# Differential attention: score products over all 128 rows, with stacked hi and lo parts, and the values of the second half among the first heads

## The chip, the cores and the metric

One core of a Trainium2 chip runs the whole kernel in one launch. The metric is the device time of that launch in microseconds (us), the median of several runs. All inputs lie in the chip's memory before the launch.

## The reference

A decoder of two layers on 512 positions with 1024 features in f32: swiglu half steps and a gated convolution in the first layer, then keys and values projected once from the residual, then a second layer with causal differential attention over them. The change touches only the attention.

```python
def diff_attention(h, k, v, w_q, lq1, lk1, lq2, lk2, g_subln, w_o, lambda_init):
    q = (h @ w_q).reshape(b, s, N_HEADS, 2, HEAD_DIM) * (HEAD_DIM ** -0.5)
    ...
    scores = jnp.einsum("bqhcd,bkhcd->bhcqk", qb, k).astype(f32)
    ...
    p = jax.nn.softmax(jnp.where(causal, scores, -jnp.inf), axis=-1)
    a = p[:, :, 0] - lam * p[:, :, 1]
    return jnp.einsum("bhqk,bkhe->bqhe", a.astype(v.dtype), v)
    ...
    o = rms_norm(o, g_subln) * (1.0 - lambda_init)
    return o.reshape(b, s, D_MODEL) @ w_o
```

There are 8 heads. Each has two components (index c) of 64 dimensions, two sets of scores and two softmaxes, whose difference is applied to values of 128 columns.

## The kernel before, in words

Activations are held transposed: features on the 128 partitions, the 512 positions along the free axis. Every f32 product is made of three matmuls of a faster type (fp32r): each operand is split into a rounded part (hi) and the rest (lo), and hi x hi, hi x lo and lo x hi are added up in PSUM. `split` (L133 on, its copy at L138 on ScalarE, its subtraction at L141 on VectorE) makes the two parts of an activation, `unit` those of a weight block: SP starts a load of 512 KB into one of two `raw` buffers (L127), ScalarE casts it to whi (L128), VectorE subtracts for wlo (L129). There are seven pairs of such buffers (`WUNITS`). `products` (L143 on) issues the three matmuls, L147 to L149.

The attention's body (L589 on) is written for one head n of eight at a time, and its functions are these. `values(half, tts)` multiplies the activations by half of the value weights, for position tiles tts (L618 to L620, 24 matmuls of 512 columns for each tile). Half 0 serves heads 0 to 3, half 1 heads 4 to 7. `keys(n, k0, k1)` makes the keys of head n, 24 matmuls of 512 columns in all, called in two halves, and at the end splits them. `queries(n)` splits the queries. `scores(n, qt)` (L639 on) makes both components' scores of the query tile qt against (qt + 1) x 128 keys: for each component three matmuls of 64 rows (L653), the first component from partitions 0 to 63, the second from 64 to 127, then a matmul that adds the mask (L655), the row maximum (`top`, L656), the exponential with its sum (L661), the reciprocal (L662) and the mixing of the two components (L665, L666) into `e`. `turn(n, qt)` transposes it on TensorE (tr, L678) and splits the result into aT. `attend(n)` multiplies by the values (L689 to L691), copies the result to `q` and squares it (osq, L694). `sub_norm(n)` adds up the squares on TensorE (otot, L698) and normalizes.

A pool `ps` of six PSUM buffers holds every sum, a pool `pst` of two the transposes and otot.

The order of the work is the order of the calls in the loop over n, except that a scheduler, when the kernel is built, may move instructions of an engine against each other; what each engine runs is then fixed. TensorE runs its instructions strictly in that order, so a matmul that waits holds all behind it. For n = 1 to 6 the calls are: half of the keys of n+1, scores(n,2), turn(n,3), attend(n-1), the other half of the keys, scores(n,1), scores(n,0), sub_norm(n-1), turn(n,2), scores(n+1,3), turn(n,1), turn(n,0). Both halves of the values and the keys of head 0 come before the loop.

Of the kernel before, what the change touches and what calls it, by code (L numbers as in the profile page):

```python
# [9 lines left out]
F32 = mybir.dt.float32  # L10
F32R = mybir.dt.float32r
# [6 lines left out]
P = 128  # L18
D = 1024
S = 512  # L20
FF = 2816
NK = D // P
NF = FF // P
NH = 8
HD = 64
# [11 lines left out]
TEMPS = 4  # L37
HALF_TEMPS = 6
RAW = 2
WARM = 9  # L40
LAMBDA_INIT = 0.8 - 0.6 * math.exp(-0.3 * 1)
MASKED = -3.0e38
# [3 lines left out]
def yoco_kernel(ctx: ExitStack, tc, i, out):  # L46
    nc = tc.nc

    const = ctx.enter_context(tc.tile_pool(name="const", bufs=1))
    xpool = ctx.enter_context(tc.tile_pool(name="xpool", bufs=1))  # L50
    apool = ctx.enter_context(tc.tile_pool(name="apool", bufs=5 * NK))
    wsp = ctx.enter_context(tc.tile_pool(name="wsp", bufs=WUNITS))
    wraw = ctx.enter_context(tc.tile_pool(name="wraw", bufs=RAW))
    mpool = ctx.enter_context(tc.tile_pool(name="mpool", bufs=1))
# [4 lines left out]
    def slot(dtype, name):  # L59
        return apool.tile([P, S], dtype, tag="a", name=name)  # L60
# [485 lines left out]
    def attention(l, h, pn, xkv):  # L546
# [23 lines left out]
        NB = S // P  # L570
# [18 lines left out]
        def body(after, then):  # L589
# [14 lines left out]

            vu = {}

            def values(half, tts):
                accs = {tt: ps.tile([P, S], F32, tag="ps", name="v_acc") for tt in tts}
                for kk in range(NK // 2):
                    if (half, kk) not in vu:  # L610
                        vu[half, kk] = unit(i["wv"][half][:, kk * 1024 : (kk + 1) * 1024], 1024)
                    uh, ul = vu[half, kk]
                    for j in range(2):
                        k = 2 * kk + j
                        for tt in tts:
                            ah, al = (z[:, tt * P : (tt + 1) * P] for z in hkv[k])
                            wh, wl = (z[:, j * S : (j + 1) * S] for z in (uh, ul))
                            nc.tensor.matmul(accs[tt], ah, wh, start=k == 0, stop=False)  # L618
# [6 lines left out]
            kacc, ku, kq, aT, mixed, pv = {}, {}, {}, {}, {}, {}  # L625

            def keys(n, k0, k1):
                if k0 == 0:
                    kacc[n] = ps.tile([P, S], F32, tag="ps", name="k_acc")
                    ku[n] = unit(i["wk"][n], 1024)  # L630
                for k in range(k0, k1):
                    products(kacc[n], [cols(ku[n], k) + tuple(hkv[k])], k == 0, k == NK - 1)
                if k1 == NK:
                    split(kq[n][2], kq[n][3], kacc[n])

            def queries(n):
                hi, lo = pair_of_units("kq")
                kq[n] = [hi[:, :S], lo[:, :S], hi[:, S:], lo[:, S:]]
                split(kq[n][0], kq[n][1], qs[n])  # L639

            def scores(n, qt):

                qh, ql, kh, kl = kq[n]
                w = (qt + 1) * P
                qq = slice(qt * P, w)
                top, neg, sums, inv = (
                    small.tile([P, 2], F32, tag=z, name=z) for z in ("top", "neg", "sums", "inv")
                )
                sc = [ps.tile([P, S], F32, tag="ps", name="sc")[:, :w] for _ in range(2)]
                for j, (q, k) in enumerate(((qh, kh), (qh, kl), (ql, kh))):  # L650
                    for cc, s in enumerate(sc):
                        r = slice(cc * HD, (cc + 1) * HD)
                        nc.tensor.matmul(s, q[r, qq], k[r, :w], start=j == 0, stop=False)  # L653
                for cc, s in enumerate(sc):
                    nc.tensor.matmul(s[:, qt * P :], ident16, mask, start=False, stop=True)  # L655
                    nc.vector.tensor_reduce(top[:, cc : cc + 1], s, axis=AX.X, op=ALU.max)  # L656
# [25 lines left out]
            def attend(n):  # L682
                oacc = ps.tile([P, S], F32, tag="ps", name="oacc")
                e0 = (n % 4) * P
                for j in range(NB):
                    vh, vl = (z[:, e0 : e0 + P] for z in v[n // 4, j])
                    ah, al = (block(z, j, j) for z in aT[n])
                    q = slice(j * P, S)
                    nc.tensor.matmul(oacc[:, q], vh, ah, start=j == 0, stop=False)  # L689
                    nc.tensor.matmul(oacc[:, q], vh, al, start=False, stop=False)  # L690
                    nc.tensor.matmul(oacc[:, q], vl, ah, start=False, stop=j == NB - 1)  # L691
                nc.scalar.copy(qs[n], oacc)
                pv[n] = temp(S, "osq")
                nc.scalar.square(pv[n], qs[n])  # L694
# [11 lines left out]
            def normed(*ns):  # L706
                for n in ns:
                    on.append(parts_of("on"))
                    split(*on[n], qs[n])

            values(0, range(NB))
            queries(0)
            keys(0, 0, NK)
            values(1, range(NB))
            scores(0, 3)
            for n in range(NH):
                more = n < NH - 1
                if more:
                    queries(n + 1)
                    keys(n + 1, 0, 4)  # L720
                scores(n, 2)
                if not more:
                    normed(4, 5)
# [1 line left out]
                turn(n, 3)  # L725
                if n > 0:
                    attend(n - 1)
                if more:
                    keys(n + 1, 4, NK)
                else:  # L730
                    wo.begin(0, range(4, 6))
                scores(n, 1)
                scores(n, 0)
# [124 lines left out]
```

## Time and profile before

| | us |
|---|---|
| median of 3 runs | 1916.08 (1915.59 to 1917.01) |
| profiled execution | 1916.25 |
| its span | 1914.5 |
| busy TensorE (PE) / its weight loads (PEld) | 1895.8 / 1602.9 |
| busy VectorE (DVE) / ScalarE (ACT) | 993.3 / 739.5 |
| the stage from the first values to the first scores of head 0 | 49.31 |
| heads 0 to 6, from scores(n,3) to scores(n+1,3) | 97.31 |

The profile comes from one execution on the chip. Busy time is the time in which an engine has an instruction in work. The ends of matmuls are modelled, so that what counts between two matmuls is the distance of their starts. In a group's row, "x56" is the number of instructions, then come their busy time, the mean length of one in ns, and the idle time ahead of them with what ended most of it. Heads 0 to 6 are 1480.02 minus 1382.71 in the windows of the trace.

### The profile page before, as it was taken

The page shows a single profiled execution, that of the slowest core. Times are in us where ns is not written, and L with a number is a line of the kernel's source. Part 1 is how long each engine was busy: PE and PEld are TensorE (multiplying, and loading weights), DVE is VectorE, ACT ScalarE, POOL GpSimd, SP SyncE. Part 2 cuts the span into 40 slices and gives each one's busy share as a digit, 9 for nine tenths or more (in the row PEclk, how much of TensorE's full clock was granted, in tenths as well). Part 3 has the DMA queues.
Part 4 walks back from the last instruction along what each step waited for, and adds up shares of the span by engine and source line. Part 5 has one row for each costly group of instructions (what it writes and reads, how often), then busy time and mean ns, then how long its engine had stood idle before and what let it go on. Part 6 is the DMA issues. An engine that isn't in the chain of part 4 may idle for free.

```text
span 1914.5 us, 24288 instructions
## 1 busy us (share of the span) xinstructions
PE 1895.8 (99%) x9780; PEld 1602.9 (84%) x9780; DVE 993.3 (52%) x1673; ACT 739.5 (39%) x1250; POOL 1.1 (0%) x8
## 2 busy tenths in 40 slices
PE   9999999999999999999999999999999999999998
PEld 8888888988898888888988888899866898888886
DVE  7423434574566334344862443457389594234345
ACT  7322222453354322222633222335289673332132
POOL 0000000000000000000000000000000000000000
PEclk9999999999999999999999999999999999999999
DMA  5432323233323323232133332322211224233331
GB/s 167 121 102 90 106 88 103 74 95 94 112 75 104 106 87 101 90 109 89 66 114 100 103 99 95 89 87 92 74 34 61 73 67 132 78 98 100 98 90 65
DMA packets 53664, 178.45 MB, mean 93 GB/s; under 512 B 6320, under 2 KB 9520, under 8 KB 53552
## 3 DMA queue, kind: packets, MB, share of 16 engines
q1 hardware_dynamic: 51632, 174.89, 29.5%
q10 hardware_dynamic: 1920, 2.02, 0.3%
q8 instruction: 77, 1.26, 0.3%
q14 instruction: 35, 0.29, 0.1%
HBM read 174.79 MB, written 2.10 MB: 92 GB/s over the span
## 4 chain that ended last, share of the span: by engine, by line
PE 89%; DVE 7%; ACT 3%; DMA 1%; issue 1%; SPq 0%; DVEq 0%; ACTq 0%
PE acc L147 26%; PE acc L148 26%; PE acc L149 26%; PE d_acc L359 2%; PE d_acc L358 2%; PE d_acc L360 2%; DVE h_lo L221 1%; DVE d L242 1%; DVE x L243 1%; PE v_acc L618 1%; PE v_acc L620 1%; PE v_acc L619 1%; DMA raw<-in_wg 1%; ACT e L661 1%; DVE top L656 1%
## 5 line engine op out<-in xcount | busy, mean ns | idle before, releaser
L147 PE MATMUL acc<-h_hi,whi 128*128 128x512 f32 (+1 forms) x1952 | 697.6, 358 | 4.4 <-ACT whi L128 2.6
L148 PE MATMUL acc<-h_lo,whi 128*128 128x512 f32 (+1 forms) x1952 | 697.6, 358 | 0.1
L149 PE MATMUL acc<-h_hi,wlo 128*128 128x512 f32 (+1 forms) x1952 | 696.3, 357 | 0.0
L128 ACT CAST whi<-raw 128x1024 fp32r<-128x1024 f32 (+2 forms) x336 | 334.4, 1019 | 867.5 <-PE acc L148 718.7
L129 DVE TENSOR_TENSOR wlo<-raw,whi 128x1024 fp32r<-128x1024 f32 (+2 forms) x336 | 396.2, 1182 | 238.8 <-ACT whi L128 237.6
L147 PEld LDWEIGHTS acc<-h_hi,whi 128*128 128x128 f32 x1952 | 367.1, 188 | 59.4 <-ACT whi L128 2.8
L148 PEld LDWEIGHTS acc<-h_lo,whi 128*128 128x128 f32 x1952 | 367.6, 188 | 54.1 <-DVE h_lo L221 0.3
L149 PEld LDWEIGHTS acc<-h_hi,wlo 128*128 128x128 f32 x1952 | 367.3, 188 | 53.7
L410 DVE TENSOR_TENSOR gs<-acc,r 128x512 f32<-128x512 f32 (+1 forms) x100 | 62.5, 625 | 443.8 <-PE acc L149 443.7
L148 PE MATMUL acc<-act_lo,whi 128*128 128x512 f32 (+1 forms) x624 | 223.7, 359 | 0.0
L149 PE MATMUL acc<-act_hi,wlo 128*128 128x512 f32 (+1 forms) x624 | 223.2, 358 | 0.0
L147 PE MATMUL acc<-act_hi,whi 128*128 128x512 f32 (+1 forms) x624 | 223.1, 358 | 0.0
L148 PEld LDWEIGHTS acc<-act_lo,whi 128*128 128x128 f32 x624 | 117.8, 189 | 18.4
L147 PEld LDWEIGHTS acc<-act_hi,whi 128*128 128x128 f32 x624 | 117.4, 188 | 18.0
L149 PEld LDWEIGHTS acc<-act_hi,wlo 128*128 128x128 f32 x624 | 117.3, 188 | 17.7
L138 ACT CAST act_hi<-us 128x512 fp32r<-128x512 f32 (+1 forms) x100 | 56.5, 568 | 64.3 <-DVE us L414 64.3
L358 PE MATMUL d_acc<-whi,act_hi 128*128 128x512 f32 x176 | 68.4, 390 | 0.0
L359 PE MATMUL d_acc<-whi,act_lo 128*128 128x512 f32 x176 | 68.4, 389 | 0.0
L360 PE MATMUL d_acc<-wlo,act_hi 128*128 128x512 f32 x176 | 68.4, 389 | 0.0
L412 DVE TENSOR_TENSOR us<-acc,r 128x512 f32<-128x512 f32 (+1 forms) x100 | 62.5, 625 | 0.0
L141 DVE TENSOR_TENSOR act_lo<-us,act_hi 128x512 fp32r<-128x512 f32 (+1 forms) x100 | 61.7, 620 | 0.7 <-ACT act_hi L138 0.7
L414 DVE TENSOR_TENSOR us<-us,gs 128x512 f32<-128x512 f32 (+1 forms) x100 | 61.5, 620 | 0.4
(156 smaller groups left out, 1646.8 us busy)
## 6 DMA issues: line engine op xcount, KB each, us to landing
raw<-in_wg SPq DMA_DIRECT2D x85, 512.0 KB, 3.8
raw<-in_wu SPq DMA_DIRECT2D x85, 512.0 KB, 3.4
raw<-in_wd SPq DMA_DIRECT2D x48, 448.0 KB, 3.4
raw<-in_wd SPq DMA_DIRECT2D x24, 512.0 KB, 3.8
raw<-in_wci SPq DMA_DIRECT2D x24, 512.0 KB, 3.5
raw<-in_wdt SPq DMA_DIRECT2D x22, 512.0 KB, 3.7
raw<-in_wco SPq DMA_DIRECT2D x8, 512.0 KB, 3.5
raw<-in_wq SPq DMA_DIRECT2D x8, 512.0 KB, 3.4
```

Source lines behind the costliest of these rows:

```text
L128: casts.append(nc.scalar.copy(hi[:, z], raw[:, z]).ins)
L129: nc.vector.tensor_tensor(lo[:, z], raw[:, z], hi.bitcast(F32)[:, z], op=ALU.subtract)
L141: nc.vector.tensor_tensor(dst_lo, src, dst_hi.bitcast(F32), op=ALU.subtract)
L147: nc.tensor.matmul(acc, wh, ah, start=first and j == 0, stop=False)
L148: nc.tensor.matmul(acc, wh, al, start=False, stop=False)
L149: nc.tensor.matmul(acc, wl, ah, start=False, stop=last and j == n - 1)
L358: nc.tensor.matmul(acc, ah, wh, start=k == 0, stop=False)
L359: nc.tensor.matmul(acc, al, wh, start=False, stop=False)
L360: nc.tensor.matmul(acc, ah, wl, start=False, stop=k == m1 - m0 - 1)
L410: nc.vector.tensor_tensor(gs, g, r2[:, p:q], op=ALU.mult)
L412: nc.vector.tensor_tensor(us, up, r2[:, p:q], op=ALU.mult)
L414: nc.vector.tensor_tensor(us, us, gs, op=ALU.mult)
```

## The change

Scores. Instead of three matmuls of 64 rows for each component, there are two of 128 rows. The fixed operand has q_hi of that component on partitions 0 to 63 and q_lo on 64 to 127; the moving operand has k_hi on both halves in its first 512 columns and k_lo on both halves in its second 512. So two matmuls give hi x hi + lo x hi and hi x lo + lo x lo: the product of the two lo parts, left out before, is now there. The stacks are made by transfers from SBUF to SBUF that SP issues (`move`): five for the keys of a head, in two rounds, since the last two overwrite what the first three read, and three for its queries. A head's keys then take two of the seven pairs of weight buffers' tiles as `kk`, and the queries take slots of `apool`, which grows from 40 to 48; `attend` writes into a new slot instead of `q`.

Order. keys(0) come ahead of values(0). The values of the second half are made one position tile at a time in heads 0 to 3: in heads 0 to 2 behind the second half of the keys, in head 3 at its start. Queries of six heads are split and moved ahead of the loop, the others in heads 0 and 1. In heads 4 to 6 all 24 key products stand at the head's start.

```diff
             def keys(n, k0, k1):
...
                 if k1 == NK:
-                    split(kq[n][2], kq[n][3], kacc[n])
+                    a, b = kk[n] = pair_of_units("kk")
+                    split(a[:, :S], a[:, S:], kacc[n])
+                    move(b[up], a[low])
+                    for dst, src in ((b[low], a[low]), (a[low], a[up])):
+                        move(dst[:, :S], src[:, S:])
+                        move(dst[:, S:], src[:, :S])
 
             def queries(n):
-                hi, lo = pair_of_units("kq")
-                kq[n] = [hi[:, :S], lo[:, :S], hi[:, S:], lo[:, S:]]
-                split(kq[n][0], kq[n][1], qs[n])
+                hi, lo = slot(F32R, "qhi"), qs[n].bitcast(F32R)
+                split(hi, lo, qs[n])
+                both = slot(F32R, "qboth")
+                move(both[up], hi[low])
+                move(both[low], lo[low])
+                move(hi[low], lo[up])
+                xs[n] = hi, both
 
             def scores(n, qt):
...
-                for j, (q, k) in enumerate(((qh, kh), (qh, kl), (ql, kh))):
-                    for cc, s in enumerate(sc):
-                        r = slice(cc * HD, (cc + 1) * HD)
-                        nc.tensor.matmul(s, q[r, qq], k[r, :w], start=j == 0, stop=False)
+                for cc, s in enumerate(sc):
+                    for j in range(2):
+                        nc.tensor.matmul(s, xs[n][cc][:, qq], kk[n][cc][:, j * S : j * S + w], start=j == 0, stop=False)
...
+            value_weights(0)
+            keys(0, 0, NK)
+            for n in range(AHEAD // 2):
+                queries(n)
             values(0, range(NB))
-            queries(0)
-            keys(0, 0, NK)
-            values(1, range(NB))
+            for n in range(AHEAD // 2, AHEAD):
+                queries(n)
             scores(0, 3)
             for n in range(NH):
                 more = n < NH - 1
+                if n == 0:
+                    value_weights(1)
+                if n == 3:
+                    values(1, [n])
                 if more:
-                    queries(n + 1)
                     keys(n + 1, 0, 4)
+                if n < NH - AHEAD:
+                    queries(n + AHEAD)
+                if n > 3 and more:
+                    keys(n + 1, 4, NK)
                 scores(n, 2)
...
-                if more:
+                if n <= 3:
                     keys(n + 1, 4, NK)
-                else:
+                if n < 3:
+                    values(1, [n])
+                if not more:
                     wo.begin(0, range(4, 6))
```

The scheduler gives some calls other places than before. On TensorE at the end of head 0, before (tr_11255 is tile 2 of head 0, tr_11287 its tile 1; sc_11265 and sc_11266 are scores(1,3), sc_11323 scores(1,2); k_acc_11300 the keys of head 2):

```order
L653 MATMUL sc_11265<-kqhi_11131 128x512
L678 MATMUL tr_11255<-ident_7887,e_11171 128x128 x3
L653 MATMUL sc_11266<-kqhi_11131 128x512
L653 MATMUL sc_11265<-kqlo_11132,kqhi_11131 128x512
...
L147 MATMUL k_acc_11300<-h_hi_10692,whi_11302 128x512
...
L149 MATMUL k_acc_11300<-h_hi_10698,wlo_11303 128x512
L653 MATMUL sc_11323<-kqhi_11131 128x384
L678 MATMUL tr_11287<-ident_7887,e_11220 128x128 x2
```

So scores(1,3) and half of the keys of head 2 stand ahead of the transposes of tile 1. The same place after the change (sc_11196 is the second component of scores(0,0), tr_11215, tr_11245 and tr_11250 are tiles 2, 1 and 0, sc_11225 and sc_11226 scores(1,3), k_acc_11254 the keys of head 2):

```order
L671 MATMUL sc_11196<-mask_7894,ident16_7892 128x128
L694 MATMUL tr_11215<-ident_7887,e_11099 128x128 x3
L694 MATMUL tr_11245<-ident_7887,e_11182 128x128 x2
L694 MATMUL tr_11250<-ident_7887,e_11206 128x128
L669 MATMUL sc_11225<-kkhi_11129,qhi_10859 128x512 x2
L669 MATMUL sc_11226<-kklo_11130,qboth_10862 128x512 x2
...
L150 MATMUL k_acc_11254<-h_hi_10692,whi_11256 128x512
```

All three transposes have moved ahead of scores(1,3). At the end of head 3, before (sc_11841 and sc_11842 are scores(4,3), tr_11831 is tile 2 of head 3, tr_11863 tile 1, otot_11820 the norm's sum of head 2):

```order
L698 MATMUL otot_11820<-osq_11752,half128_92 128x512
L678 MATMUL tr_11831<-ident_7887,e_11720 128x128 x3
L653 MATMUL sc_11841<-kqhi_11680 128x512
L653 MATMUL sc_11842<-kqhi_11680 128x512
...
L147 MATMUL k_acc_11876<-h_hi_10692,whi_11878 128x512
...
L653 MATMUL sc_11899<-kqhi_11680 128x384
L678 MATMUL tr_11863<-ident_7887,e_11785 128x128 x2
```

and after (otot_11862, the transposes of tiles 2, 1 and 0, and sc_11883 and sc_11884, which are scores(4,3)):

```order
L715 MATMUL otot_11862<-osq_11791,half128_92 128x512
L694 MATMUL tr_11873<-ident_7887,e_11758 128x128 x3
L694 MATMUL tr_11903<-ident_7887,e_11829 128x128 x2
L694 MATMUL tr_11908<-ident_7887,e_11853 128x128
L669 MATMUL sc_11883<-kkhi_11805,qhi_10996 128x512
L669 MATMUL sc_11884<-kklo_11806,qboth_10999 128x512 x2
```

Here too the transposes of tiles 1 and 0 now stand ahead of the next head's scores; between heads 1 and 2 and between heads 2 and 3 they do not.

More of the change, by code (lines that the diff above doesn't have):

```diff
@@ L39 @@
 RAW = 2
+SCRATCH = 512
+SLOTS = 48
+AHEAD = 6
 WARM = 9
@@ L50, in yoco_kernel @@
     xpool = ctx.enter_context(tc.tile_pool(name="xpool", bufs=1))
-    apool = ctx.enter_context(tc.tile_pool(name="apool", bufs=5 * NK))
+    apool = ctx.enter_context(tc.tile_pool(name="apool", bufs=SLOTS))
     wsp = ctx.enter_context(tc.tile_pool(name="wsp", bufs=WUNITS))
@@ L605, in body, with value_weights @@
             vu = {}
+            def value_weights(half):
+                for kk in range(NK // 2):
+                    vu[half, kk] = unit(i["wv"][half][:, kk * 1024 : (kk + 1) * 1024], 1024)
             def values(half, tts):
@@ L609, in values @@
                 for kk in range(NK // 2):
-                    if (half, kk) not in vu:
-                        vu[half, kk] = unit(i["wv"][half][:, kk * 1024 : (kk + 1) * 1024], 1024)
                     uh, ul = vu[half, kk]
@@ L623, in values @@
                     split(*v[half, tt], accs[tt])
-            kacc, ku, kq, aT, mixed, pv = {}, {}, {}, {}, {}, {}
+            kacc, ku, kk, xs, aT, mixed, pv = {}, {}, {}, {}, {}, {}, {}
+            up, low = slice(0, HD), slice(HD, P)
+            move = lambda dst, src: nc.sync.dma_start(dst.bitcast(F32), src.bitcast(F32))
             def keys(n, k0, k1):
@@ L633, in keys @@
                 if k1 == NK:
-                    split(kq[n][2], kq[n][3], kacc[n])
-            def queries(n):
-                hi, lo = pair_of_units("kq")
-                kq[n] = [hi[:, :S], lo[:, :S], hi[:, S:], lo[:, S:]]
-                split(kq[n][0], kq[n][1], qs[n])
+                    a, b = kk[n] = pair_of_units("kk")
[4 more added lines that the diff above has]
+                        move(dst[:, S:], src[:, :S])
+            def queries(n):
+                hi, lo = slot(F32R, "qhi"), qs[n].bitcast(F32R)
[5 more added lines that the diff above has]
+                xs[n] = hi, both
             def scores(n, qt):
-                qh, ql, kh, kl = kq[n]
                 w = (qt + 1) * P
@@ L691, in attend @@
                     nc.tensor.matmul(oacc[:, q], vl, ah, start=False, stop=j == NB - 1)
+                qs[n] = slot(F32, "o")
                 nc.scalar.copy(qs[n], oacc)
@@ L845 @@
     arrays = {f"in_{k}": np.ascontiguousarray(v) for k, v in arrays.items()}
-    nc = bacc.Bacc("TRN2", target_bir_lowering=False, num_devices=1)
+    nc = bacc.Bacc("TRN2", target_bir_lowering=False, num_devices=1, dynamic_dma_scratch_size=SCRATCH)
     aps = {
```

## The prediction

> **What bounds the kernel now.** The page is read first: busy time of each engine, then the shares of the chain that ended last.
>
> ```profile
> PE 1895.8 (99%) x9780; PEld 1602.9 (84%) x9780; DVE 993.3 (52%) x1673; ACT 739.5 (39%) x1250; POOL 1.1 (0%) x8
> PE 89%; DVE 7%; ACT 3%; DMA 1%; issue 1%; SPq 0%; DVEq 0%; ACTq 0%
> ```
>
> TensorE (PE) is the bound, and 89% of the chain is its own work. A microsecond of PE work or PE idle is a microsecond of the run; VectorE (DVE) and ScalarE (ACT) matter only where PE waits for them. The windows view, cut where scores(n,3) start, gives heads 0 to 6 (columns: window, length and busy PE, PEld, DVE, ACT, POOL, granted clock, DMA share, GB/s).
>
> ```profile
> 1382.71:1394.03 11.32, 10.98 (x65) 7.49 (x64) 8.78 (x20) 7.58 (x17) 0.00 (x0) 1.00 0.15 47
> 1394.03:1407.98 13.95, 13.95 (x80) 9.79 (x80) 11.40 (x34) 10.97 (x30) 0.00 (x0) 1.00 0.12 39
> 1407.98:1422.31 14.33, 13.72 (x82) 9.61 (x81) 12.37 (x38) 12.44 (x34) 0.00 (x0) 1.00 0.11 37
> 1422.31:1436.64 14.33, 13.92 (x81) 9.87 (x80) 12.53 (x35) 12.03 (x33) 0.00 (x0) 1.00 0.13 38
> 1436.64:1451.04 14.40, 13.97 (x82) 9.89 (x81) 13.40 (x36) 13.13 (x35) 0.00 (x0) 1.00 0.11 38
> 1451.04:1465.99 14.95, 13.78 (x80) 9.73 (x79) 14.91 (x40) 13.98 (x35) 0.00 (x0) 1.00 0.28 87
> 1465.99:1480.02 14.03, 13.97 (x83) 9.82 (x82) 12.43 (x34) 12.68 (x34) 0.00 (x0) 1.00 0.18 58
> ```
>
> DVE and ACT are 80 to 99% busy from head 1 on: a head's softmax takes almost as long as its matmuls. The groups of PE over these heads and the waits view say how little PE loses to that so far.
>
> ```profile
> L678 PE MATMUL tr<-ident,e 128*128 128x128 f32 x67 | 12.2, 283 | 2.3 <-DVE aT_lo L141 1.9 <-DVE e L666 0.2
> L698 PE MATMUL otot<-osq,half 128*128 128x512 f32 x12 | 6.6, 628 | 0.7 <-ACT osq L694 0.7
> PE tr L678 <- DVE aT_lo L141: 1.9, 4, 0.6
> ```
>
> Idle is 3.0 us in seven heads. Ends of matmuls are modelled: one of 512 columns is shown .40 long though the next starts .23 later (rows below), so each of a dozen stalls hides up to .17; 3.0 to 5.0 is the honest figure, about .7 a head.
>
> **The shorter score products.** The timeline of PE shows a call of 512 columns, one of 256, and attend, whose matmuls use all 128 rows (start, us).
>
> ```profile
> 1404.88 0.40 PE L149 MATMUL k_acc<-h_hi,wlo 128*128 128x512 f32 x1
> 1405.20 0.39 PE L653 MATMUL sc<-kqhi 64*128 64x256 f32 x2
> 1405.76 0.28 PE L655 MATMUL sc<-mask,ident 128*128 128x128 bf16 x2
> 1405.97 0.33 PE L653 MATMUL sc<-kqhi 64*128 64x128 f32 x2
> 1406.46 0.29 PE L655 MATMUL sc<-mask,ident 128*128 128x128 bf16 x2
> 1407.56 0.49 PE L678 MATMUL tr<-ident,e 128*128 128x128 f32 x3
> 1407.98 0.50 PE L653 MATMUL sc<-kqhi 64*128 64x512 f32 x2
> 1408.32 0.40 PE L653 MATMUL sc<-kqlo,kqhi 64*128 64x512 f32 x2
> 1408.88 0.29 PE L655 MATMUL sc<-mask,ident 128*128 128x128 bf16 x2
> 1415.92 0.40 PE L691 MATMUL oacc<-aT_hi,v_lo 128*128 128x512 f32 x1
> 1416.15 0.34 PE L689 MATMUL oacc<-aT_hi,v_hi 128*128 128x384 f32 x1
> 1416.68 0.28 PE L689 MATMUL oacc<-aT_hi,v_hi 128*128 128x256 f32 x1
> 1416.80 0.28 PE L690 MATMUL oacc<-aT_lo,v_hi 128*128 128x256 f32 x1
> 1417.20 0.28 PE L691 MATMUL oacc<-aT_hi,v_lo 128*128 128x128 f32 x1
> 1417.31 0.44 PE L149 MATMUL k_acc<-h_hi,wlo 128*128 128x512 f32 x1
> ```
>
> A full-row matmul takes its columns: .23 for 512, .12 for 256, .11 for 128. Before, the two components run side by side in rows 0 to 63 and 64 to 127 (the x2 rows), so a call has three slots and not six; but entering the 64-row form costs extra: from 1408.32 minus 1407.98 the first pair takes .34, not .23, and 1404.88 plus .23 leaves .09 before 1405.20. After, a call has four full slots.
> - 512: before 1407.56 + 3 x .11 = 1407.89 to 1408.88, .99; after 4 x .23 = .93. Saves .06.
> - 256: 1405.11 to 1405.76, .65; after 4 x .12 = .48. Saves .17.
> - 128: .49 plus about .08 of entering, .57; after .45. Saves .12. 384: .10, an estimate between its neighbours.
>
> That is .45 a head, 3.4 us in eight heads, plus some .6 us where transposes split a call before and the form is left and entered once more (three calls, .11 + .09 each, an estimate): **-4.0**. If the entering cost belonged to the masks and not the rows, little would be left: 0 to -4.
>
> A rule speaks against this part. The Trainium skill, TensorE: Matmul & The Clock Gate, Measured speedup vs the span model, gives a pack of row tiles one matmul's duration plus about 4 ns for each further tile; by it each call goes from three slots to four, +.23 +.17 (between its neighbours) +.12 +.11 a head, about +5 us in all. The trace agrees on the side-by-side pairs and adds the entering cost, which the rule lacks.
>
> **The values of the second half.** The same 96 products of .23 (22 us) go from ahead of the heads into heads 0 to 3, 24 (5.5 us) each. No work is saved; what they can earn is the old stalls there. In heads 1 and 2 they stand between scores(n,2) and scores(n,1) and give DVE and ACT time: stalls of .7 go, in head 0 also, and in head 3 they are replaced: 4 x .7 = **-2.8** (1.7 by the idle column alone).
>
> **The new order at the end of heads 0 and 3.** Before, scores(n+1,3) and half of the key products stood between the softmax of scores(n,1), scores(n,0) and its transposes. After, all three transposes are ahead of scores(n+1,3). This row and the small operations' prices show what they wait for.
>
> ```profile
> 1412.60 0.41 PE L678 MATMUL tr<-ident,e 128*128 128x128 f32 x2 [0.61 <-DVE aT_lo L141]
> L656 DVE TENSOR_REDUCE top<-sc 128x1 f32<-128x256 f32 x16 | 6.2, 416 | 1.1 <-PE sc L655 1.1
> L661 ACT ACTIVATE e<-sc,neg 128x256 f32<-128x256 f32 x16 | 7.5, 480 | 0.1
> L665 ACT ACTIVATE e<-e,nl 128x256 f32<-128x256 f32 x8 | 4.1, 517 | 0.5 <-DVE inv L662 0.4
> L666 DVE SCALAR_TENSOR_TENSOR e<-e,inv 128x256 f32<-128x256 f32 x8 | 3.9, 484 | 0.4 <-ACT e L665 0.2
> ```
>
> From the mask of scores(1,1) (1405.76) to its transposes (1412.60) lie 6.8 us, queues and other work included. The chain's own large operations make .42 + 2 x .48 + .52 + .48 = 2.4. So a transpose of tile 1 can start 2.4 to 6.8 us behind its mask. What PE has to do meanwhile in the new order:
> - Head 0: scores(0,0), .54, and tile 2's transposes, .33: .9. Stall 1.5 to 5.9. DVE and ACT have only the two chains there, so I take a chain of 4.4, nearer to the lower end's row with the small operations added: **+3.5**.
> - Head 3: the same .9 and otot, .4 (an estimate, under the modelled .63 of its row): 1.3. Stall 1.1 to 5.5. Head 2's norm work is queued on both engines, as at 1412.60, and the third transpose needs the buffer that otot holds until it is read: **+4.3**, near the upper row. Even with a quick chain this one stays, since the keys' stacks land late here (below).
>
> Heads 1 and 2 keep scores(n+1,3) and the keys in between. In heads 4 to 6 the 24 key products now stand in one piece at the head's start, so less is left behind attend: otot waits for osq in head 4, 0 to 2 us, taken **+1.5**; head 6 0 to 2.5, taken **+.9**.
>
> **The stacks.** 64 more DMAs on SP, 8 for each head. No transfer inside SBUF is in this trace; the nearest rows are a transfer out of SBUF and a weight load.
>
> ```profile
> out_x<-fg SPq DMA_DIRECT2D x8, 256.0 KB, 2.0
> raw<-in_wk SPq DMA_DIRECT2D x8, 512.0 KB, 3.5
> ```
>
> Keys move in two rounds (the second reads what the first must have read), with the split ahead (about 1.3) and a weight load that may be queued between: 1.3 + 2 x 2.0 = 5.3 to 5.3 + 3.5 = 8.8 us from the last key product to scores(n+1,3). In heads 0 to 2 the cover is the value block, 5.5, two score calls with masks, 1.2, and transposes, over 7.5 with the stall of head 0; in heads 4 to 6 two to three score calls and attend, about 6. Between heads 3 and 4 it is only 1.2 + 1.3, but the stall of 4.3 there waits beside it. I take **0**; bounds 0 to +1.5 in each of heads 3 to 6. Behind a move that waits on SP stand weight loads that are needed a head later; at a DMA share of .11 to .28 that costs nothing.
>
> **The start of the stage.** keys(0) now stand where the first values stood; their third product needs wlo of the third weight load.
>
> ```profile
> 1333.66 0.39 PE L618 MATMUL v_acc<-whi,h_hi 128*128 128x512 f32 x1
> 1334.14 1.22 DVE L129 TENSOR_TENSOR wlo<-raw,whi 128x1024 fp32r<-128x1024 f32 x1
> ```
>
> That wlo ends at 1335.36, the third product could start at 1333.66 + .45 = 1334.11: +1.25; with the later h_lo parts, due every .7 us and not every 2.8, **+1.5**, at most 2.5.
>
> **Sum.** -4.0 - 2.8 + 3.5 + 4.3 + 1.5 + .9 + 0 + 1.5 = +4.9. On the profiled execution's 1916.25 that is 1921.2; the median of the runs lies .17 lower, so **1921**. What a measurement here tells from no change is .2%, 3.8 us: 1912.2 to 1919.9 count as no change.
>
> **Rivals.**
> 1. *The softmax gets through by itself, faster.* With 5.5 us of values in each of four heads, DVE and ACT are no longer near full there; chains run at their own 2.4, the stalls are 1.5 and 1.1, and no head from 4 on loses (-2.1 of old stalls too, since the keys in one piece cover the transposes): -4.0 - 2.8 - 2.1 + 1.5 + 1.1 + 1.25 = -5.1, 1911. It decides from tile 1's transposes within 2.4 us of their mask. For it: heads 0 and 1 show 8.8 and 11.4 of DVE, the lowest. Against: the 6.8 of 1412.60. Chance .18.
> 2. *Half-sized stalls.* 1.8 and 2.2, the rest as taken: +1.0, 1917. Chance .20.
> 3. *The stacks land late.* SP holds a weight load between the rounds, and scores(n+1,3) wait, say 1.0 in each of heads 3 to 6 (within the bounds above): 4.9 + 4.0 = 8.9, 1925. Against: the cover of 6. Chance .12.
> 4. *The clock.* The longest wait of PE for another engine in these heads is .7 (the otot row), and every window has a clock of 1.00, so no row shows what a stall of 3.5 to 4.3 does. If the clock halved for the twelve key products behind each of the two, that is 2 x 12 x .23 = 5.5 more: 1926. Chance .05. The Trainium skill, TensorE: Matmul & The Clock Gate, Why this matters for your kernels, warns of idle gaps over some 3 us, after which PE is back at half clock; no run here shows it so far.
> 5. *The change doesn't pay even in slots:* three slots to four without any entering cost saved, by the .23 to .11 above: 4.9 + 4.0 + 5.0 = +14, 1930. Against: the .09 and .11 rows. Chance .03.
>
> The forecast itself, 1919 to 1924, has .42. Slower than .2%: .42 less a little, .12, .05, .03, in all .59. Within: .20 and .04 of rivals' edges, .24. Faster: rival 1 less its edge, .17. The range for 8 in 10 takes in rivals 1 to 4: 1911 to 1926.
>
> **What would show it.** Four score slots per call with no extra at either end; PE idle of 3.5 and 4.3 in front of the transposes of heads 0 and 3, released by e or aT_lo; heads 1 and 2 at about 18 us, the 19.5 and 19.8 that 13.95 and 14.33 plus 5.5 make, less 1.5. Idle in front of a score product, released by a DMA, speaks for rival 3; clock below 1.00 for rival 4. A head 0 of at most 16.8 (11.32 + 5.5), or no stall over 2 us at the transposes, would prove the forecast wrong.

## The result, and the profile after

| | before | after |
|---|---|---|
| median, us | 1915.84 (4 runs, 1915.41 to 1917.01) | 1935.34 (4 runs, 1932.50 to 1938.06) |
| ratio | | 1.0096, 95% interval 1.0084 to 1.0108 |
| profiled execution, us | 1916.25 | 1935.19 |
| its span, us | 1914.5 | 1933.4 |

The kernel is slower by 19 us. The direction was the one forecast; the size was outside the range (1911 to 1926). One correction to the words on the change: the moving operand of each component holds k_hi above and k_lo below in its first 512 columns, and k_lo above and k_hi below in its second. The sum over both products is as told there.

The page of the changed kernel first:

```profile
PE 1896.6 (98%) x9716; PEld 1608.8 (83%) x9716; DVE 996.8 (52%) x1673; ACT 739.9 (38%) x1250; POOL 1.1 (0%) x8
...
PE 87%; DVE 7%; DMA 2%; ACT 2%; issue 1%; SPq 0%; DVEq 0%; ACTq 0%
```

PE is as long busy as before, with 64 matmuls fewer, and the span grew by 19: idle time came, and, as will be seen, work at a slower clock. Heads 0 to 6 in the windows view, cut at the starts of scores(n,3) as before:

```profile
1363.27:1382.71 19.44, 15.83 (x84) 12.71 (x82) 15.53 (x37) 12.71 (x32) 0.00 (x0) 0.98 0.75 191
1382.71:1401.77 19.06, 19.05 (x96) 15.37 (x94) 9.42 (x23) 8.07 (x18) 0.00 (x0) 0.93 0.28 76
1401.77:1421.54 19.77, 18.68 (x99) 14.74 (x98) 13.62 (x38) 13.67 (x38) 0.00 (x0) 1.00 0.26 68
1421.54:1446.18 24.64, 19.19 (x99) 15.05 (x100) 16.62 (x46) 16.41 (x44) 0.00 (x0) 0.94 0.21 54
1446.18:1463.31 17.13, 14.95 (x69) 11.06 (x69) 9.62 (x26) 9.01 (x25) 0.00 (x0) 0.88 0.30 77
1463.31:1479.98 16.67, 14.39 (x73) 10.80 (x73) 13.46 (x36) 12.42 (x34) 0.00 (x0) 0.93 0.31 80
1479.98:1497.41 17.43, 13.79 (x75) 10.78 (x73) 14.44 (x34) 12.90 (x28) 0.00 (x0) 0.97 0.38 98
```

Against before plus the 5.5 us of values in heads 0 to 3 (16.8, 19.5, 19.8, 19.8, then 14.4, 15.0, 14.0) that is +2.6, -.4, -.1, +4.8, +2.7, +1.7 and +3.4. The clock column is new: before it was 1.00 in every row. The last 4 us of the 19 lie outside these heads: 1.35 ahead of the stage (the first product of keys(0) starts at 1335.01, the first of values(0) before at 1333.66; in the eighteen kernels below, whose earlier stages are the same, that place varies from 1332.0 to 1336.5, so it is not the change's), 1.2 at the start of the stage and 1.5 behind the start of scores(7,3).

The waits view names engines:

```profile
PE tr L694 <- DVE e L682: 6.6, 2, 3.6
PE otot L715 <- ACT osq L711: 5.2, 3, 2.0
PE sc L669 <- DMA kkhi<-kkhi: 2.3, 3, 1.0
...
PE oacc L705 <- ACT aT_hi L141: 2.0, 3, 1.2
PE tr L694 <- DVE n_q L184: 1.8, 1, 1.8
...
PE sc L669 <- DVE neg L673: 1.1, 1, 1.1
```

Read so, the softmax chain (e, osq, n_q) costs 14 us and the transfers 2. The rows of SP, of the DMA queues and of the first product of scores(3,3) say something else:

```profile
1414.12 1.84 SPq L632 DMA_DIRECT2D kklo<-kkhi  x3
1416.84 0.34 SPq L130 DMA_DIRECT2D raw<-in_wk  x1
1418.12 1.11 SPq L632 DMA_DIRECT2D kkhi<-kkhi  x2
```

```profile
kklo<-kkhi SPq DMA_DIRECT2D x16, 128.0 KB, 2.4
kklo<-kkhi SPq DMA_DIRECT2D x8, 256.0 KB, 2.9
kkhi<-kkhi SPq DMA_DIRECT2D x16, 128.0 KB, 3.8
```

```profile
1421.54 0.47 PE L669 MATMUL sc<-kkhi,qhi 128*128 128x512 f32 x1 [1.09 <-DVE neg L673]
```

The first round takes 4.2 us, since SP issues its three transfers one after the other (the last lands at 1418.27). The second round (kkhi) is issued 4.0 us after the first: each of its transfers waits for the one of the first round that reads its target, and is issued within .1 us of that landing for n = 1, 2, 4, 5 and 6. A weight load of 512 KB stands ahead of it. It lands at 1421.45 (first) and 1421.71: scores(3,3) start at 1421.54, and the view puts the wait down to an operation of DVE, which had ended at 1420.64. From the landing times of the trace, for every head (last key product's end; last landing; start of scores(n,3)):

```
n   last key product   stack landed   scores(n,3) start   product to landing
1        1370.92          1381.65          1382.71              10.7
2        1394.15          1401.88          1401.77               7.7
3        1412.56          1421.71          1421.54               9.2
4        1437.43          1446.36          1446.18               8.9
5        1454.93          1463.57          1463.31               8.6
6        1470.62          1479.40          1479.98               8.8
7        1487.49          1498.87          1497.41              11.4
```

(The first product reads only what the first of the last two transfers brings, so a start can be some .3 before the last landing; for n = 7 the second product waited 1.0 more.) For n = 3, 4, 5 and 7 the start lies .04 to .13 behind the landing of that first one. For n = 2 PE had work up to the start (head 1 is busy for 19.05 of 19.06), so that landing cost nothing there. For n = 1 and 6 the start is 1.1 and .6 behind the last landing; without the waits ahead of tr and otot it could have come hardly more than that sooner. So most of the idle time ahead of tr and otot lies in the shadow of the landing.

The clock: behind the stall of head 0 the same products take twice as long.

```profile
1378.07 0.50 PE L694 MATMUL tr<-ident,e 128*128 128x128 f32 x3
1382.18 0.88 PE L694 MATMUL tr<-ident,e 128*128 128x128 f32 x3 [3.61 <-DVE e L682]
1382.71 1.20 PE L669 MATMUL sc<-kkhi,qhi 128*128 128x512 f32 x2
1383.71 1.05 PE L669 MATMUL sc<-kklo,qboth 128*128 128x512 f32 x2
1384.57 0.44 PE L671 MATMUL sc<-mask,ident 128*128 128x128 bf16 x2
```

```profile
1382.70:1385.20 2.50, 2.50 (x9) 1.79 (x8) 0.89 (x3) 0.54 (x2) 0.00 (x0) 0.50 0.23 52
...
1446.18:1450.20 4.02, 4.02 (x10) 2.61 (x11) 2.19 (x4) 0.14 (x1) 0.00 (x0) 0.50 0.00 0
...
1477.60:1481.00 3.40, 3.39 (x8) 2.09 (x9) 1.49 (x7) 3.24 (x12) 0.00 (x0) 0.51 0.16 36
```

A call of 512 columns takes 1.86 to its mask where four slots are .93. Three times the clock is at .50, for 2.5, 4.0 and 3.4 us of work: half of 9.9 is 5 us, an estimate.

The score products themselves came out as the change meant them. A call of 256 columns at full clock:

```profile
1437.05 0.39 PE L152 MATMUL k_acc<-h_hi,wlo 128*128 128x512 f32 x1
1437.27 0.40 PE L669 MATMUL sc<-kkhi,qhi 128*128 128x256 f32 x2
1437.51 0.40 PE L669 MATMUL sc<-kklo,qboth 128*128 128x256 f32 x2
1437.75 0.28 PE L671 MATMUL sc<-mask,ident 128*128 128x128 bf16 x2
```

It enters without a gap (1437.05 to 1437.27) and has four slots of .12: .48, as forecast, against .65.

### The profile page after: what moved, and what is told of

It is laid out like the page before. It is cut to its first block, busy times and chain, and to the rows that moved or that the text cites. A ratio compares the mean times of both kernels' runs of the same rounds, so it can differ in the third digit from the quotient of the medians.

```text
span 1933.4 us, 24270 instructions
## 1 busy us (share of the span) xinstructions
PE 1896.6 (98%) x9716; PEld 1608.8 (83%) x9716; DVE 996.8 (52%) x1673; ACT 739.9 (38%) x1250; POOL 1.1 (0%) x8
## 4 chain that ended last, share of the span: by engine, by line
PE 87%; DVE 7%; DMA 2%; ACT 2%; issue 1%; SPq 0%; DVEq 0%; ACTq 0%
PE acc L152 25%; PE acc L150 25%; PE acc L151 24%; PE d_acc L362 2%; PE d_acc L361 2%; PE d_acc L363 2%; DVE h_lo L224 1%; DVE d L245 1%; DVE x L246 1%; DVE wlo L132 1%; PE sc L669 1%; PE k_acc L150 1%; PE k_acc L152 1%; PE k_acc L151 1%; PE v_acc L624 1%; PE v_acc L623 1%
```

## The experiments

Times are medians, each with its ratio to runs of the kernel before on the same chip; these had medians of 1916.25 to 1917.17.

**First set: transfers or order.**

*no_moves.*

```diff
-                    move(b[up], a[low])
-                    for dst, src in ((b[low], a[low]), (a[low], a[up])):
-                        move(dst[:, :S], src[:, S:])
-                        move(dst[:, S:], src[:, :S])
+                    kk[n] = a, a
```

and likewise without the moves of the queries.

> The changed kernel without the 64 transfers: both components read the unstacked parts, hi and lo of queries and keys as split (so the scores are other numbers, of the same size and number of products). Theory A (the transfers cost, because the next head's scores wait for them and so the transposes were put ahead of those scores): the stalls of heads 0 and 3 (3.6, 3.0 and 1.8) and the half clock behind them go, 1914 to 1920. Theory B (the new places of values and keys cost, whatever the scores read): 1930 or more. The forecast's own terms without heads 0 and 3: 1916.25 + 4.9 - 7.8 = 1913.

1914.16 us, ratio .9987 (.9977 to .9996). In this program the scheduler leaves scores(1,3) and scores(4,3) ahead of the transposes of tiles 1 and 0.

```profile
1363.67:1378.52 14.85, 14.85 (x80) 12.25 (x79) 11.26 (x24) 9.58 (x21) 0.00 (x0) 1.00 0.11 37
...
1415.72:1434.16 18.44, 18.43 (x100) 14.60 (x98) 12.17 (x35) 12.57 (x32) 0.00 (x0) 1.00 0.00 1
1434.16:1446.71 12.55, 12.37 (x71) 9.51 (x68) 11.26 (x29) 10.38 (x28) 0.00 (x0) 1.00 0.14 42
```

Heads 0, 3 and 4 take 14.9, 18.4 and 12.6 and not 19.4, 24.6 and 17.1, with PE idle for .2 us at most and at full clock. Theory A holds: without the stacks the scheduler does not move the transposes, and the stalls are not there. This kernel also keeps what else the change has, the larger `apool` and another size of the DMAs' scratch (`SCRATCH`), so these are not what costs.

*order_only.* The changed kernel with the three 64-row products for each component, and `split(*kk[n], kacc[n])` with no moves.

> The changed kernel's order of work (keys of head 0 first, values of the second half in heads 0 to 3, queries ahead, keys in one piece from head 4 on), with the score products of before (64 rows, three for each component) and no transfers. Theory A: about 4 above no_moves, as the score products save 4.0: 1918 to 1924. Theory B: 1932 or more. If the 64-row form costs nothing to enter: at most the time of no_moves, by up to 5 less.

1920.24, ratio 1.0016 (1.0007 to 1.0026): 6.1 above no_moves, where 4 was expected, and 3.1 above before. The score products' own rows (groups of instructions, 1360 to 1512) have 15.0, 11.7 and 11.2 us of PE here and 17.2 and 16.1 in no_moves: 4.6 more for three slots of 64 rows than for four full ones, .14 in each of 32 calls. The rest of the 6.1 is not in these rows.

*stack_only.* The changed kernel with the lines from `values(0, ...)` to the end of the loop as before the change.

> Only the score products over 128 rows with their transfers; values, queries and keys where they were before. Theory A: between the last key product and scores(n+1,3) lie only some 2.5 us, and the stack needs 5 to 9, so 3 to 5 us in each of seven heads, with a half clock behind each: 1930 to 1945. Theory B: the transfers are hidden, 1912 (1916 - 4.0).

1959.44, ratio 1.0221 (1.0205 to 1.0236), 14 above the upper end of what was expected. Head 2's end:

```profile
1437.02 0.69 PE L694 MATMUL tr<-ident,e 128*128 128x128 f32 x2 [4.46 <-DVE n_q L184]
```

```profile
1437.50:1443.00 5.50, 5.50 (x17) 4.12 (x17) 3.52 (x9) 2.09 (x6) 0.00 (x0) 0.54 0.24 88
```

4.5 us of waiting (timeline), then 5.5 us at .54 of the clock (windows); the windows of heads 1 to 3 have a mean clock of .84 to .86. Here, too, the wait is put down to n_q, while the stacks of heads 2, 3 and 4 land at 1418.24, 1437.76 and 1458.14 and scores(n,3) start at 1417.99, 1437.51 and 1457.48. In this place n_q does end at 1436.97, .05 ahead of the transposes that stand before the scores, so this trace alone can't tell the chain from the landing. Without the values as cover the kernel loses 42 us and not 19.

*filled.*

```diff
+                for _ in range(FILL.get((n, qt), 0)):
+                    nc.tensor.matmul(tr.rearrange("p a b -> p (a b)"), hkv[0][0][:, :P], hkv[0][0], start=True, stop=True)
```

> The changed kernel with products of no use in the idle time of heads 0 and 3, ahead of the transposes of tiles 1 and 0 (15 in head 0; 12 and 7 in head 3, of .23 each), whose results are written over. If the clock halves after an idle time of some 3 us: the half clock behind head 0's stall (1382 to 1385, 1.6 us lost) and behind head 3's (1443 to 1450, 2 to 3 lost) goes, 3 to 4 us less than the changed kernel, 1931. If it doesn't, or if the half clock has another cause: the same 1935 or more.

1934.11, ratio 1.0085 (1.0068 to 1.0102): too near to 1935 to decide by the time. In head 3 the first twelve of these products waited 2.5 us themselves and then took 4.1 us, most of it at half clock, and five more stand behind scores(4,3); that head became longer (26.0). In head 0 they went where they were meant to go, and there the clock stays up and head 1 falls from 19.06 to 17.82, with head 0 at 19.32 (19.44):

```profile
1379.56:1382.00 2.44, 2.44 (x13) 1.87 (x13) 1.79 (x4) 0.45 (x2) 0.00 (x0) 1.00 0.23 54
1382.00:1385.00 3.00, 3.00 (x17) 2.48 (x16) 1.23 (x6) 2.03 (x5) 0.00 (x0) 1.00 0.00 0
```

So that one half clock is worth 1.2 us, which is half of the 2.5 us of work at .50.

**Second set: is it the landing?**

*one_round.*

```diff
-                    split(a[:, :S], a[:, S:], kacc[n])
-                    move(b[up], a[low])
-                    for dst, src in ((b[low], a[low]), (a[low], a[up])):
-                        move(dst[:, :S], src[:, S:])
-                        move(dst[:, S:], src[:, :S])
+                    for z, part in ((a, up), (b, low)):
+                        split(z[part, :S], z[part, S:], kacc[n][part])
+                    move(a[low], a[up])
+                    move(b[up], b[low])
```

> The changed kernel with the stacks of the keys made in one round: each half of the keys is split straight into its place (two casts and two subtractions of 64 rows instead of one each of 128), and two transfers that wait for nothing else fill the other halves. Theory A2 (the landing of the stack sets the start of scores(n+1,3) in every head from 1 to 6, as the landings and the starts lie within 0.1 us): landing some 4 us sooner, the waits go, 1914 to 1920, with up to 4 us for the added splits. Theory C (the softmax chain, osq and the PSUM buffers named by the waits cost, and the landing only coincides): VectorE and ScalarE have 1.3 us more in each head, 1930 or more.

1920.99, ratio 1.0025 (1.0015 to 1.0034), 1 above the stated end. From the last key product to the landing lie 5.9 to 9.3 us (7.7 to 11.4 in the changed kernel). 15 us of the 19 are gone, although DVE and ACT have more to do. Theory C falls. In this program, as in no_moves, scores(1,3) and scores(4,3) stand ahead of the transposes of tiles 1 and 0 again: the scheduler's order goes with the landing.

*half_ahead.* stack_only with `keys(n + 1, 4, NK)` at the start of head n and `keys(n + 2, 0, 4)` behind attend.

> stack_only with the keys half a head earlier: the second half of the keys of n+1 at the start of head n, the first half of n+2 behind attend; values where they were before; transfers in two rounds. Theory A2: 8 to 9 us of work lie between the last key product and scores(n+1,3), the stack of 7 to 8 us is mostly hidden, the score products save 4 to 6: 1911 to 1916. Theory C: the order around the softmax is like stack_only, 1940 or more.

1926.62, ratio 1.0051 (1.0036 to 1.0066): 33 less than stack_only, but 10 above what was expected. The stacks of heads 1 to 7 land 9.7 to 12.4 us after the last product there, in heads 1 to 6 still with the starts of scores(n,3) (1428.52 and 1428.28 for n = 3), with waits of 1.2 and less.

*half_ahead_one.* The same with one round.

> half_ahead with the stacks of the keys in one round, as in one_round. Theory A2: the landing is hidden in both, so within 2 us of half_ahead, 1910 to 1916; if half_ahead still waits for its landing, this one is lower by that. Theory C: above half_ahead by the added splits, up to 10.

1926.95, ratio 1.0053 (1.0038 to 1.0068): as half_ahead. The waits for landings have gone from the view, but oacc now waits 6.4 us for aT_hi: this order has another limit behind the landing, in the transposes.

*moves_unread.*

```diff
-                    a, b = kk[n] = pair_of_units("kk")
-                    split(a[:, :S], a[:, S:], kacc[n])
+                    a, b = pair_of_units("kk")
+                    kk[n] = [(slot(F32R, "khi"), slot(F32R, "klo"))] * 2
+                    hi, lo = kk[n][0]
+                    split(hi, lo, kacc[n])
+                    for z, r in ((a, up), (b, low)):
+                        for s in (up, low):
+                            move(z[s, :S], hi[r])
+                            move(z[s, S:], lo[r])
```

> The changed kernel with the transfers made but read by nobody: the keys' parts go to slots, the score products read those for both components (other numbers than the reference's, same number and size of products), and eight transfers a head copy them into the stacks. Theory A2: only the wait for the landing costs, not the transfers: as no_moves, 1913 to 1918. Rival D (the transfers cost by themselves: SP's queue delays the weight loads, or the traffic does): 1922 or more.

1920.51, ratio 1.0017 (1.0008 to 1.0026), between the two. The 6 us above no_moves are not at the scores: the view has key products waiting for their weights (k_acc <- wlo 3.0, <- whi 1.5), head 1 takes 23.1. The likeliest reading, not tried by itself, is that eight transfers a head on SP's queue delay the weight loads behind them. In the changed kernel, with five, key products wait .8 in all.

**Third set: stacks without a DMA, and the clock.**

*pool_stacks.*

```diff
-                    move(b[up], a[low])
-                    for dst, src in ((b[low], a[low]), (a[low], a[up])):
-                        move(dst[:, :S], src[:, S:])
-                        move(dst[:, S:], src[:, :S])
+                    nc.gpsimd.tensor_copy(b[low], a[low])
+                    nc.gpsimd.tensor_copy(b[up], a[low])
+                    nc.gpsimd.tensor_copy(a[low], a[up])
```

> The changed kernel with the stacks of the keys made by three copies on GpSimd, which is idle, instead of five transfers: no trip over a DMA queue, one split as before, no more work for ScalarE and VectorE. Theory A2 (the landing of the stack is what costs): some 4 to 6 us sooner in each head, 1914 to 1919, at or under the time before. Theory C (softmax chain, osq, buffers): 1928 or more.

1922.71, ratio 1.0036 (1.0021 to 1.0051): 13 gone, 4 above the stated end: for n = 1 to 7 the copies end 5.5 to 6.8 us behind the last key product, 1.6 to 4.6 sooner than the transfers, where 4 to 6 sooner was expected. One head's end, GpSimd and PE:

```profile
1431.30 1.04 POOL L644 CAST kklo<-kkhi 64x1024 fp32r<-64x1024 f32 x1 [19.11 <-DVE kkhi L144]
...
1432.38 1.04 POOL L645 CAST kklo<-kkhi 64x1024 fp32r<-64x1024 f32 x1
1433.49 1.91 POOL L646 CAST kkhi<-kkhi 64x1024 fp32r<-64x1024 f32 x1
...
1435.45 0.73 PE L668 MATMUL sc<-kkhi,qhi 128*128 128x512 f32 x2 [3.40 <-POOL kkhi L646]
```

With the copies on an engine, the wait bears the right name. Head 3 takes 22.1; heads 0 to 2, which have the values as cover, 15.0, 18.8 and 18.4, as no_moves.

*pool_half.* pool_stacks with `keys(n + 1, 4, NK)` behind attend in every head.

> pool_stacks with the keys of heads 4 to 6 in two halves, as before the change. If the keys in one piece cost by themselves, as the prediction had it (otot waits, 1.5 and .9), 2.4 less than pool_stacks. If otot's waits there came with the stack's landing only: the same within 1.5.

1927.89, ratio 1.0063 (1.0045 to 1.0081), 5 above pool_stacks: neither of the two. The keys in one piece do not cost; they give the stacks of heads 5 to 7 cover, and in halves scores(n,3) wait 9.7 us in three heads for GpSimd (5.7 in pool_stacks).

*pool_stack_only.* stack_only with the same three copies.

> stack_only (values, queries and keys where they were before) with the stacks of the keys made by GpSimd. Theory A2: stack_only's 42 us go but for what three copies (2 to 3 us) exceed the 2.5 us of cover by, up to 1 in each of seven heads, less the 4.8 to 6.2 us that the score products save: 1911 to 1919. Theory C: 1940 or more.

1947.89, ratio 1.0165 (1.0149 to 1.0181), far above, and by the time alone in the range of theory C. The waits name the copies:

```profile
PE sc L668 <- POOL kkhi L646: 18.1, 6, 4.2
```

From the last key product to the end of the copies lie 5.0 to 6.5 us, and scores(n,3) start .05 behind that end in every head from 1 on, 18.1 us of waiting in six heads; the clock over heads 0 to 6 is .91 in the mean. The cover was rightly known; the copies had been taken at 2 to 3 and last 3.5 to 4.5, and the first starts 1.6 to 2.0 behind the last key product.

*stack_filled.*

```diff
+                    for _ in range(FILL):
+                        nc.tensor.matmul(spare[n], hkv[0][0][:, :P], hkv[0][0][:, P:], start=True, stop=True)
                     scores(n + 1, 3)
```

> stack_only with 16 products of no use (384 columns, .175 each, 2.8 us) ahead of scores(n+1,3) in heads 0 to 6, where TensorE is idle for 3 to 5 us; they write columns that nothing reads. If idle time halves the clock for some 6 us behind it (stack_only's windows show .50 there), 7 times up to 3 us come back: 1938 to 1946. If the half clock has another cause: 1957 to 1963.

1958.69, ratio 1.0224 (1.0208 to 1.0240). It tells nothing: the added products waited themselves for the exponentials that read the same buffer (19.8 us in seven waits), so that PE idled ahead of them.

*stack_filled_2.*

```diff
+                for _ in range(FILL if qt == 2 and n < NH - 1 else 0):
+                    nc.tensor.matmul(tr[:, 3, :], hkv[0][0][:, :P], hkv[0][0][:, :P], start=True, stop=True)
```

> stack_only with 28 products of no use (128 columns, .11 each, 3.1 us) right behind the transposes of tile 2 in heads 0 to 6, into a block of their PSUM buffer that nothing reads, so that TensorE works through most of the 4.5 us for which it waits there. If idle time brings the half clock (stack_only: .54 over 5.5 us of work behind one such wait, 2.5 us lost, six or seven times): 15 us less, 1941 to 1948. If the half clock has another cause or hides behind the landing: 1957 to 1962.

1965.07, ratio 1.0248 (1.0232 to 1.0264): 15 less was expected, and it became 6 more. The trace shows why it is no test: a rest of idle time is left, and that is enough for the clock.

```profile
1441.92 1.19 PE L670 MATMUL sc<-kkhi,qhi 128*128 128x512 f32 x2 [1.86 <-DMA kkhi<-kkhi]
```

```profile
1441.00:1442.00 1.00, 0.08 (x1) 0.11 (x1) 1.00 (x3) 0.43 (x2) 0.00 (x0) 0.50 0.96 182
1442.00:1444.00 2.00, 2.00 (x7) 1.26 (x7) 1.44 (x3) 0.00 (x0) 0.00 (x0) 0.50 0.62 236
...
1446.00:1447.00 1.00, 1.00 (x4) 0.81 (x3) 0.02 (x1) 1.00 (x3) 0.00 (x0) 0.50 0.00 0
```

The clock went to .50 within these 1.86 us without work and stayed there from 1440.8 to 1447.6. And with PE busy until 1440, the wait now carries its cause: the landing.

**Fourth set: cover.**

*values_behind.* `values(1, [n])` behind the second half of the keys for n = 3 as well.

> The changed kernel with the values of head 3 behind the second half of its keys, as in heads 0 to 2, not at its start. Theory A2: the stack of head 4 then has 5.5 us more cover, head 3 loses its 4.8 and the half clock behind it (about 2): 1927 to 1931. If head 3's loss is the softmax chain's: 1933 or more.

1927.58, ratio 1.0062 (1.0047 to 1.0077), as theory A2 had it. Head 3 takes 18.8 and not 24.6.

*values_behind_pool.* The same with GpSimd's copies.

> values_behind with the stacks of the keys made on GpSimd, 5.5 to 6.5 us from the last key product to the end. Theory A2: head 3 as head 2 (18.4, in pool_stacks 22.1), heads 4 to 6 as in pool_stacks: 1922.7 - 3.7 - the half clock behind head 3: 1917 to 1919. Otherwise 1922 or more.

1917.70, ratio 1.0006 (.9996 to 1.0015), as expected. Heads 0 to 3 take 15.0, 18.8, 18.4 and 18.4: where 5.5 us of values lie between keys and scores, copies of 4 us are hidden.

*two_ahead.* Keys of n + 2 in head n.

> The changed kernel with the keys two heads ahead (the keys of head 1 before the loop, those of n+2 in head n, values behind attend in heads 0 to 3, part of the output products in head 6), transfers in two rounds as in the change. Theory A2: a stack has a whole head to land in, nothing waits for it, and the time is that of no_moves give or take the new order: 1912 to 1918. If something other than the landing costs: 1922 or more.

1940.16, ratio 1.0124 (1.0109 to 1.0139): a miss. The stacks land 6 us and more ahead of the scores that read them, so that nothing waits for them; but in head 0 key products wait 7.8 us for their weights and a transpose 6.4, and that head takes 32.7. SP issues the load of these weights (in_wk) only at 1381.70, behind transfers and the loads of the values' weights, the last of them at 1377.30. The run tells nothing of the landing's price.

*mixed.* values_behind_pool with the 64-row products and no stacks in heads 5 to 7, and the keys of heads 4 to 6 in halves.

> values_behind_pool with the score products of before (64 rows, no stacks) in heads 5 to 7 and the keys of heads 4 to 6 in two halves. Theory A2: up to the scores of head 4 as values_behind_pool (98.8 us from the stage's first product; before 103.0), behind them as before (102.8; values_behind_pool 108.8): 1912 to 1914, under the time before. If the late heads' loss has another cause than their stacks: 1917 or more.

1915.30, ratio .9991 (.9982 to 1.0000). The stage reaches scores(4,3) 98.8 us after its first product, as expected; from there to its last output product it takes 106.5, not 102.8. By its ratio it is 1.7 us faster than before, and the interval ends at no change; the time lies between what the two theories had.

*mixed_keys.* `values(0, range(2))`, then keys(0), then the rest of the values.

> mixed with the keys of head 0 between two halves of the first values, where the weights of the keys are long there. The wait for wlo at the stage's start (.5 to .8 idle, 1.2 in all) goes: 1911 to 1913. If that wait only moves: as mixed.

1919.81, ratio 1.0013 (1.0005 to 1.0022), worse: a key product waits 2.5 us for its weights in head 0, and that head takes 20.3. Keys ahead of all values are the better place.

## Why the prediction was wrong

It had the sign, and most of the places, and missed 14 of 19 us. The sign was in part luck: it came from stalls that were put down to the new order, and the same order of calls with the new products but without the stacks (no_moves) is 2.5 to 3 us faster than before.

The step that failed is the one on the stacks: "I take **0**". Its own bounds were 5.3 to 8.8 us from the last key product to the landing against covers of 7.5, 6 and 2.5. The trace has 7.7 to 11.4: 2.0 for a round was taken from a single transfer out of SBUF, but the first round is three transfers in a row and takes some 4 us, and a transfer of the second takes 3.8. Even so the bounds overlapped the covers, and zero was the lower end's value. Without the transfers the changed kernel takes 21 to 22.5 us less, each against its own runs of before (medians +19.5 and -3.0, ratios 1.0096 and .9987): the stacks are the whole loss, and more. Rival 3 was the right mechanism, at .12, and was priced at 1 us a head where no_moves against the changed kernel shows 4.6, .3, 1.3, 6.2, 4.6, 3.6 and 1.5 in heads 0 to 6, the half clock included.

The other steps:
- *Heads 0 and 3, +3.5 and +4.3.* The stalls came, 3.6 as sized and 3.0 + 1.8 + .7 = 5.5 in place of 4.3. The waits ahead of the transposes are the softmax chain's, as forecast (in head 0 from the mask at 1377.37 to 1382.18, 4.8 us where 4.4 was taken), but the chain is not what made them cost: no_moves and one_round show that the transposes stood ahead of the scores because of the late stacks, and the landing would have held scores(1,3) to within 1.1 us of where they started. "Even with a quick chain this one stays, since the keys' stacks land late here" was said for head 3 alone; it holds for the ends of heads 2, 4 and 6 as well.
- *Heads 4 and 6, +1.5 and +.9 (head 5 nothing).* Heads 4 to 6 lost 2.7, 1.7 and 3.4. otot waits in heads 4 to 6 (1.1, 2.0 and 2.0), but not because of the keys in one piece: no_moves has them too, there otot stands behind the first products of scores(n+1,3) and waits for nothing, and in pool_half keys in two halves are slower. In the changed kernel the landing sets the end of heads 4 and 6, and in head 5 comes within .6.
- *Score products, -4.0.* Right in mechanism, and nearly in size: 4.6 by the products' own rows in order_only and no_moves, 6.1 by the two medians. The rule of the row-tile pack in the Trainium skill (TensorE: Matmul & The Clock Gate, Measured speedup vs the span model), by which four slots for three would cost 5, does not hold here: it lacks what entering the 64-row form costs, by these numbers some .3 a call (an estimate: .14 saved and .16 for the fourth slot).
- *Values, -2.8.* Less than half of it at best. order_only, with the values among the heads and no stacks, takes 15.7, 19.7, 19.8 and 19.5 in heads 0 to 3 against 16.8, 19.5, 19.8 and 19.8, 1.2 less, and as a whole is 3.1 us slower than before; heads 1 and 2 gain nothing. No run moves the values alone.
- *Start of the stage, +1.5.* 1.2: 28.26 from the first product to scores(0,3) against 49.05 less 22.0 (49.05 counts from the first product of the values at 1333.66; the 49.31 of the table ahead counts from 1333.40).
- *Rival 4, the clock, .05.* It happened, three times, for 5 us in all (worked out from the rows; 1.2 for the first is measured). The row on which the chance rested (no wait over .7) was one of the profile of before; the stalls that the same text forecast, 3.5 and 4.3, should have raised it. The Trainium skill, TensorE: Matmul & The Clock Gate, Why this matters for your kernels, was right in kind; but in stack_filled_2 the clock fell within an idle time of 1.86 us, and in pool_stacks behind one of 1.20.

Still open: how much of the second round's 3.8 us is the weight load queued ahead of it (no run took that load away); what the landing costs by itself and what the order that the scheduler chose around it (no run keeps that order and takes away the landing alone, and in the changed kernel chain and landing end so close to each other that taking away either one alone would give back some 2 to 4 us, an estimate from the waits and landings above); and why from the scores of head 4 on the orders tried here need more than before even without a late stack: to the last output product 104.8 in no_moves and 106.5 in mixed, 102.8 before.

## What to carry to other kernels

When operands are built by transfers, compare the whole way from the last producer to the landing with the work between, head by head, and take the cost at its middle rather than at zero where the two overlap. Then look up when transfers landed: a start that coincides with a landing in head after head points to it, even if the waits view names an operation that stands ahead in the queue, and a run in which the landing comes sooner tells. And where stalls of several microseconds are forecast, the half clock behind them belongs in the sum.

## What the runs showed of the hardware

- The granted clock fell to .50 in stretches of one length or a multiple of it: in the changed kernel from 1381.91 to 1385.33, 1443.36 to 1450.18 and 1477.49 to 1480.90 (3.4, 6.8 and 3.4 us), the starts 61.45 and 34.13 apart, which is 18 and 10 times 3.41 (the trace's records of the clock; the windows view has .50 in each of these stretches).
- The length of an idle time alone does not decide. Idle time of 1.20 us (pool_stacks, to 1449.60) was followed by half clock at 1450.41; one of 2.04 ahead of otot in head 6 of the changed kernel and one of 2.86 in stack_filled (to 1521.94) left the clock at 1.00.
- A transfer of 128 KB within SBUF took 2.4 us, one of 256 KB 2.9, and one of 128 KB behind a weight load of 512 KB 3.8 (medians, in the changed kernel). SP takes .5 to .7 us to issue one, so three in a row took some 4.
- GpSimd's first copy of 64 x 1024 f32, within the same partitions, takes 1.04 us in pool_stacks; the second and third, to other partitions, take 1.03 to 1.98, 1.6 in the mean.
